# Hybrid decoder trunk: the sum over experts starts at zero, and each expert's rows bring half of the residual

## Chip, cores and metric

The kernel runs on one core of a Trainium2 chip. The metric is the device time of one execution in microseconds (us), the median over runs; all times here come from the profiler of the chip or from those runs.

## What is computed

The program is a decoder trunk of two layers over 512 tokens (four row tiles of 128) and 1024 columns, in float32. Each layer has a mixer with three kinds of attention (called `mix` here), a post-norm, a mixture of experts and a second post-norm:

```
for l in range(DEPTH):                       # DEPTH = 2, alpha = (2*DEPTH)**0.25
    mix = hybrid_mixer(x, ...)
    x = layer_norm(alpha * x + mix, ln1_g[l], ln1_b[l])
    moe = hier_moe(x, ...)                   # one group of 4, two experts of its 8
    x = layer_norm(alpha * x + moe, ln2_g[l], ln2_b[l])

# hier_moe, per token t, over 32 experts:
h = silu(t @ w_gate[e]) * (t @ w_up[e])      # 1024 -> 256
y = y + (h * gate[e]) @ w_down[e]            # 256 -> 1024; gate is zero but for two experts
```

Each token has exactly two experts with a gate that is not zero.

## The kernel before, in words

**Weights.** One expert has 3 MB of weights: two units of 1.5 MB, which `load_next` (L517 to L530) fetches with SP's DMA queue. Thirteen such units of SBUF form a ring; some of them (letters T and m of the ring, and the unit inside `xroom`) lie in rooms that attention used before. The ring is filled in the course of attention and the router; a further unit can only be loaded when the products that read its old content are done.

**End of attention.** For each of four row tiles, `out_proj` (its DVE instruction is L865) adds the output projection to the scaled residual in `yn[i]`. Statistics give mean and reciprocal deviation, ACT normalises the tile in place (L919), and ACT's queue writes it to `xd` in DRAM (L920). These rows are normalised, but without gain and bias.

**`first_rows`** (L885 to L890) then makes the residual of the second half of the layer: two VectorE (DVE) products over 128x1024, times the gain and plus the bias of the first norm (both in the tile `gb1`), and a DMA of 512 KB on ACT's queue into `y2` in DRAM. It works in place in `yn[i]`, so it waits until the DMA to `xd` has read that tile; only the fourth tile has a room of its own. It runs four times per layer. All experts add to `y2` later.

**Router** (L930 to L1098). A chain of small DVE instructions takes the best group (`gm`, `ghot`), the two best experts (`hot`, `selb`), the position of each token in its expert's list (`posm`) and one-hot rows (`oneh`, L1054); TensorE (PE) turns these into lists (`lists`), and `slot_rows` (L981 to L988) into row numbers `ri`.

**Pairs.** Two experts with up to 64 tokens each make a pair; there are 16 pairs per layer. GpSimd (POOL) gathers the 128 rows of a pair from `xd` by an indirect DMA into one of two rooms (`gathered`, DMA at L1000). `turned` (PE at L1011, DVE and ACT at L1017 and L1015) transposes them in eight PE instructions and applies gain and bias of the first norm on the way out of PSUM. 32 up products (`experts_up`), SiLU on ACT and a DVE product (`h`, L1032), two transposes and 16 down products (`experts_down`) follow. The two halves of the result leave PSUM scaled by the gate, one on ACT (L1044) and one on DVE (L1045), into one of three rooms (`row_room`), and POOL scatters the rows with an indirect DMA that adds to `y2` (L1046).

In the loop, `turned` of the next pair stands after `experts_mid` of the present pair and before its `experts_down`; the gather for two pairs later follows it. An `overflow` loop after the 16 pairs takes tokens beyond the 64 of an expert; in this profile it runs one item in layer 2 and none in layer 1.

**Second norm.** `gb2 = norm_rows(1)` (L243) loads gain and bias of the second norm, 1 MB broadcast, into the same tile as `gb1`. It stands in the text after pair 3, but the scheduler has put its DMA early on SP's queue, between weight loads (the order is shown below). After the last pair `y2` is read back (L1251), and the second norm uses `gb2` (L1263, L1265).

The scheduler keeps each engine's own stream in order: an instruction that waits holds all behind it on the same engine or queue.

Of the kernel before, what the change touches and what calls it, by code (L numbers as in the profile page):

```python
# [7 lines left out]
F32 = mybir.dt.float32  # L8
# [3 lines left out]
AF = mybir.ActivationFunctionType  # L12
# [52 lines left out]
def trunk(tc, a, out, dbg=None):  # L65
# [4 lines left out]
    with es:  # L70
# [177 lines left out]
        for l in range(DEPTH):  # L248
# [286 lines left out]

            dp = xhp.tile([128, 2 * NK * S], F32, name="dp", tag="xh")
# [366 lines left out]
            for i in range(NT):  # L903
# [17 lines left out]
                if i:  # L921
                    first_rows(i - 1)
# [96 lines left out]

            halves_ = ((0, 64), (64, 128))  # L1020

            def experts_up(xg, w):
                gu = bank("S")
                for k in range(NK):
                    for j, (c0, c1) in enumerate(halves_):
                        mm(gu[c0:c1], xg[:, k, c0:c1], gate_up(w[j], k), k == 0, k == NK - 1)
                return gu

            def experts_mid(gu):
                h = cp.tile([128, FH], F32, name="h", tag="rwg")  # L1030
                A.activation(h, gu[:, 0:FH], AF.Silu)  # L1031
                V.tensor_tensor(h, h, gu[:, FH:2 * FH], OP.mult)  # L1032
                return h

            def experts_down(h, w, rows):
# [13 lines left out]
            RI, XR, XG = {}, {}, {}  # L1049
# [49 lines left out]
            first_rows(NT - 1)  # L1099
# [4 lines left out]
            XG[0] = turned(XR.pop(0))  # L1104
# [31 lines left out]
            def overflow():  # L1136

                n_items = nc.values_load(eidi[0:1, MAX_ITEMS:MAX_ITEMS + 1], min_val=0, max_val=MAX_ITEMS)
                with tc.For_i(0, n_items) as item:
# [66 lines left out]
                    y = row_room()  # L1206
                    A.activation(y[0:64, 0:512], o[0:64], AF.Copy, scale=wr[0:64])
                    V.tensor_scalar(y[0:64, 512:1024], o[64:128], wr[64:128], None, op0=OP.mult)
# [3 lines left out]
            for p in range(NE // 2):  # L1212
# [9 lines left out]
                st = experts_down(h, w, RI.pop(p))  # L1222
# [9 lines left out]
            with tc.issue_after(last_on["PE"].ins), tc.issue_after(last_on["A"].ins), tc.issue_after(last_on["V"].ins), tc.issue_after(st.ins):  # L1232
# [12 lines left out]
            for j in range(2):  # L1245
                yu = carve(unit("A", "yt"), 0, [2, D])
# [8 lines left out]
            for i in range(NT):  # L1255
# [6 lines left out]
                for t, c in zip(src, halves):  # L1262
                    V.scalar_tensor_tensor(z[:, c], t, mv[:, 0:1], gb2[:, 0, c], op0=OP.subtract, op1=OP.mult)  # L1263
                for c in halves if i in (0, 3) else [slice(0, 1024)]:
                    V.scalar_tensor_tensor(z[:, c], z[:, c], mv[:, 2:3], gb2[:, 1, c], op0=OP.mult, op1=OP.add)  # L1265
# [77 lines left out]
```

## Time and profile before

| | us |
|---|---|
| runs | 1380.25, 1386.83, 1387.82 (median 1386.83) |
| profiled execution | 1385.0 |
| its span, first to last instruction | 1383.2 |

| engine | busy us | share of the span |
|---|---|---|
| PE (matmul) | 1194.4 | 86% |
| DVE | 696.6 | 50% |
| ACT | 442.9 | 32% |
| POOL | 292.5 | 21% |

In the rows further down, L888 is line 888 of the kernel; `yn<-yn,gb` names what an instruction writes and reads. SPq and ACTq are the DMA queues of SP and ACT. A bracket such as [4.74 <-DMA xd<-yn] gives the time for which the engine stood idle before the instruction, and what ended that. In views by stretches, the five busy times stand in the order PE, PEld (weight loads of PE), DVE, ACT, POOL; PEclk is the granted clock as a share of 2.4 GHz, and DMA the mean busy share of the 16 DMA engines.

### The profile page before, as it was taken

The page shows a single profiled execution, that of the slowest core. Times are in us where ns is not written, and L with a number is a line of the kernel's source. Part 1 is how long each engine was busy: PE and PEld are TensorE (multiplying, and loading weights), DVE is VectorE, ACT ScalarE, POOL GpSimd, SP SyncE. Part 2 cuts the span into 40 slices and gives each one's busy share as a digit, 9 for nine tenths or more (in the row PEclk, how much of TensorE's full clock was granted, in tenths as well). Part 3 has the DMA queues.
Part 4 walks back from the last instruction along what each step waited for, and adds up shares of the span by engine and source line. Part 5 has one row for each costly group of instructions (what it writes and reads, how often), then busy time and mean ns, then how long its engine had stood idle before and what let it go on. Part 6 is the DMA issues. An engine that isn't in the chain of part 4 may idle for free. (4 is left out here: it accounts for less than half of the span.)

```text
span 1383.2 us, 18273 instructions
## 1 busy us (share of the span) xinstructions
PE 1194.4 (86%) x6701; PEld 815.8 (59%) x6708; DVE 696.6 (50%) x1822; ACT 442.9 (32%) x1050; POOL 292.5 (21%) x286
## 2 busy tenths in 40 slices
PE   6989999999939989887599999999996699898860
PEld 6989976668924533222398899666795343332320
DVE  7599638684552422111668892668636333211125
ACT  3362256673102221111235322857611122111100
POOL 5332431201001121100332334230000122111011
PEclk9999999999969999999799999999998799999985
DMA  7321440115397999998552224200426899999943
GB/s 240 116 80 51 128 158 11 36 40 185 118 402 279 400 413 405 409 390 287 166 165 78 65 83 140 98 23 22 156 104 247 347 384 407 409 403 410 356 166 123
DMA packets 63898, 293.81 MB, mean 212 GB/s; under 512 B 16064, under 2 KB 20672, under 8 KB 48192
## 3 DMA queue, kind: packets, MB, share of 16 engines
q1 hardware_dynamic: 52128, 267.43, 50.5%
q0 software_dynamic: 9376, 16.81, 4.9%
q10 hardware_dynamic: 2304, 8.39, 1.5%
q8 instruction: 54, 0.88, 0.3%
q14 instruction: 36, 0.29, 0.1%
HBM read 278.06 MB, written 31.82 MB: 224 GB/s over the span
## 5 line engine op out<-in xcount | busy, mean ns | idle before, releaser
L97 PE MATMUL acc<-U,xh 128*128 128x384 f32 (+1 forms) x1584 | 298.9, 343 | 18.9 <-DVE xh L212 7.0
L97 PEld LDWEIGHTS acc<-U,xh 128*128 128x128 f32 x1584 | 280.5, 193 | 21.9 <-issue 6.9
L97 PE MATMUL S<-w,xg 128*64 128x512 f32 (+1 forms) x968 | 272.0, 608 | 10.6 <-DMA w<-w_e 8.9
L97 PEld LDWEIGHTS S<-w,xg 128*64 128x64 f32 x968 | 83.1, 141 | 138.8 <-issue 112.9
L1017 DVE TENSOR_SCALAR xg<-acc,lv 128x128 f32<-128x128 f32 x128 | 45.8, 404 | 179.6 <-PE S L97 142.9
L97 PE MATMUL o<-w,hT 128*64 128x512 f32 x488 | 125.4, 603 | 5.9 <-ACT hT L90 3.4
L199 POOL TENSOR_TENSOR U<-raw,U 128x768 fp32r<-128x768 f32 (+2 forms) x46 | 90.3, 1967 | 166.9 <-ACT U L196 166.9
L1046 POOL DMA_INDIRECT y<-xroom,ri x32 | 51.4, 1607 | 294.8 <-DVE xroom L1045 180.5
L1031 ACT ACTIVATE h<-S 128x256 f32<-128x256 f32 x32 | 12.3, 383 | 270.6 <-PE S L97 270.6
L196 ACT ACTIVATE U<-raw 128x768 fp32r<-128x768 f32 (+2 forms) x88 | 68.0, 812 | 71.6 <-PE acc L97 43.7
L1045 DVE TENSOR_SCALAR xroom<-o,rv 128x512 f32<-128x512 f32 x32 | 24.0, 751 | 117.7 <-PE o L97 117.7
L97 PEld LDWEIGHTS o<-w,hT 128*64 128x64 f32 x488 | 39.2, 138 | 67.1 <-issue 57.4
L1000 POOL DMA_INDIRECT xroom<-xd,ri x33 | 35.2, 1066 | 180.5 <-PE acc L1011 94.5
L199 DVE TENSOR_TENSOR U<-raw,U 128x768 fp32r<-128x768 f32 (+2 forms) x42 | 52.8, 1260 | 36.5 <-ACT U L196 34.0
L1011 PEld LDWEIGHTS acc<-cst,xroom 128*128 128x128 f32 x256 | 29.4, 147 | 60.6 <-issue 36.0
L90 ACT ACTIVATE uc<-T 128x512 f32<-128x512 f32 (+3 forms) x117 | 51.3, 460 | 40.9 <-PE T L297 39.1
L1015 ACT ACTIVATE xg<-acc,lv 128x128 f32<-128x128 f32 x128 | 48.9, 458 | 45.5 <-PE T L97 35.8
L1011 PE MATMUL acc<-cst,xroom 128*128 128x128 f32 x256 | 43.7, 298 | 22.7 <-DMA xroom<-xd,ri 20.7
L97 PE MATMUL acc<-U,oh 128*128 128x384 f32 (+1 forms) x384 | 63.3, 315 | 0.0
L1044 ACT ACTIVATE xroom<-o,rv 128x512 f32<-128x512 f32 x32 | 22.0, 687 | 111.0 <-PE o L97 111.0
L97 PEld LDWEIGHTS acc<-U,oh 128*128 128x128 f32 x384 | 56.8, 189 | 1.2 <-issue 1.0
L403 DVE MATCH_REPLACE8 uc<-m,uc 128x256 f32<-128x256 f32 (+2 forms) x96 | 51.4, 539 | 0.0
(367 smaller groups left out, 1942.0 us busy)
## 6 DMA issues: line engine op xcount, KB each, us to landing
w<-w_e SPq DMA_DIRECT2D x110, 1536.0 KB
raw<-w_in SPq DMA_DIRECT2D x64, 384.0 KB
xroom<-w_e SPq DMA_DIRECT2D x8, 1536.0 KB
w<-w_e SPq DMA_DIRECT2D x24, 512.0 KB
raw<-w_o SPq DMA_DIRECT2D x16, 384.0 KB
gb<-ln_rows SPq DMA_DIRECT2D x4, 1024.0 KB
xd<-yn ACTq DMA_DIRECT2D x8, 512.0 KB
y<-yn ACTq DMA_DIRECT2D x6, 512.0 KB
```

The costliest lines, as they stand in the source:

```text
L90: A.activation(o, i, AF.Copy, scale=1.0 if scale is None else scale)
L97: return PE.matmul(o, l, r, start=start, stop=stop, skip_group_check=True)
L196: A.activation(hi, r, AF.Copy)
L199: e.tensor_tensor(lo, r, hi.bitcast(F32), OP.subtract)
L403: V.match_replace(out=acc_t[i][:, :n], in_to_replace=m8, in_values=acc_t[i][:, :n], imm_value=TAKEN)
L1000: G.indirect_dma_start(out=xr[0:n], out_offset=None, in_=xd, in_offset=bass.IndirectOffsetOnAxis(ap=ri[0:n], axis=0), bounds_check=S - 1, ...
L1011: PE.transpose(t[:, 128 * j:128 * j + 128], xr[:, 128 * k:128 * k + 128], ident)
L1015: A.activation(xg[:, k], o, AF.Identity, scale=lv[:, 0, k, 0:1], bias=lv[:, 0, k, 1:2])
L1017: V.tensor_scalar(xg[:, k], o, lv[:, 0, k, 0:1], lv[:, 0, k, 1:2], op0=OP.mult, op1=OP.add)
L1044: last_on["A"] = A.activation(y[:, 0:512], o[0], AF.Copy, scale=rows[1])
L1045: last_on["V"] = V.tensor_scalar(y[:, 512:1024], o[1], rows[1], None, op0=OP.mult)
L1046: return G.indirect_dma_start(out=y2, out_offset=bass.IndirectOffsetOnAxis(ap=rows[0], axis=0), in_=y, in_offset=None, bounds_check=S - 1, ...
```

## The change

It does seven things.

1. `y2` is set to zero: POOL clears a 128x512 tile, and one SP DMA of 2 MB copies it over all of `y2`. This stands in the text after the first weight load, and in SP's order after the eighth load of attention's weights past the small norm tables, in each layer.
2. `gb1` is multiplied by 0.5 on ACT once per layer, 128x2048.
3. `first_rows` is gone, with its four calls.
4. `half_rows` is new: for each pair, two DVE products over 128x1024 make half of the residual from the gathered rows, in the room that the result will take. A token is gathered by two experts, so two halves add up.
5. Both halves of a pair's result now leave PSUM on DVE, in an instruction that also adds them to that room (`scalar_tensor_tensor`, 128x512).
6. `turned` of the next pair is issued after the last up product of the present pair, `half_rows` of the next pair after `h` of the present one, and the gather for two pairs later after that.
7. `gb2` comes in two DMAs of 512 KB after the last expert's weights, into units of the ring; the `overflow` loop uses `half_rows` on its 64 rows too.

```diff
+            y2 = dr.tile([S, D], F32, name="y2", tag="y2")
+            none = ring("P")
+            G.memset(none, 0.0)
+            SP.dma_start(y2.rearrange(...), none.unsqueeze(1).to_broadcast([128, 2 * NT, 512]))
...
             gb1 = norm_rows(0)
-            y2 = dr.tile([S, D], F32, name="y2", tag="y2")
-            def first_rows(i):
-                z = yn[i] if i < NT - 1 else at.tile([128, D], F32, name="x1", tag="u", bufs=3)
-                V.tensor_tensor(z, yn[i], gb1[:, 0], OP.mult)
-                V.tensor_tensor(z, z, gb1[:, 1], OP.add)
-                A.dma_start(y2[128 * i:128 * i + 128, :], z)
+            A.activation(gb1.rearrange("p a d -> p (a d)"), gb1.rearrange("p a d -> p (a d)"), AF.Copy, scale=0.5)
...
                 A.dma_start(xd[128 * i:128 * i + 128, :], z)
-                if i:
-                    first_rows(i - 1)
...
+            def half_rows(xr, n=128):
+                y = row_room()
+                V.tensor_tensor(y[0:n], xr[0:n], gb1[0:n, 0], OP.mult)
+                V.tensor_tensor(y[0:n], y[0:n], gb1[0:n, 1], OP.add)
+                return y
+            def next_half(p1):
+                if p1 in XR:
+                    with tc.issue_after(last_on["h"].ins):
+                        HR[p1] = half_rows(XR.pop(p1))
+                    fetch(p1 + 2)
...
                 transposes(hT.rearrange("p a b -> p (a b)"), [h[:, 0:128], h[:, 128:256]], 128)
+                next_half(p1)
...
-                y = row_room()
-                last_on["A"] = A.activation(y[:, 0:512], o[0], AF.Copy, scale=rows[1])
-                last_on["V"] = V.tensor_scalar(y[:, 512:1024], o[1], rows[1], None, op0=OP.mult)
+                for n in range(2):
+                    c = slice(512 * n, 512 * n + 512)
+                    last_on["V"] = V.scalar_tensor_tensor(y[:, c], o[n], rows[1], y[:, c], op0=OP.mult, op1=OP.add)
...
-            first_rows(NT - 1)
...
-            XG[0] = turned(XR.pop(0))
+            XG[0], HR[0] = turned(XR[0]), half_rows(XR.pop(0))
...
                 if p + 1 < NE // 2:
-                    XG[p + 1] = turned(XR.pop(p + 1))
-                    fetch(p + 3)
+                    with tc.issue_after(last_on["up"].ins):
+                        XG[p + 1] = turned(XR[p + 1])
...
-                    gb2 = norm_rows(1)
...
+            yus = [unit("A", "yt") for _ in range(2)]
+            gb2 = [yu[:, 2 * D:3 * D] for yu in yus]
+            for j in range(2):
+                SP.dma_start(gb2[j], a["ln_rows"][l:l + 1, 1, j].to_broadcast([128, D]))
```

SP's queue at the start of the experts of layer 1, before (`w` and `xroom` are weight units, `gb` the tile of both norms):

```order
L530 DMA w<-w_e 128x3072 x3
L530 DMA xroom<-w_e 128x3072
L530 DMA w<-w_e 128x3072
L243 DMA gb<-ln_rows 128x2048
L530 DMA w<-w_e 128x3072 x12
```

and with the change:

```order
L530 DMA w<-w_e 128x3072 x3
L530 DMA xroom<-w_e 128x3072
L530 DMA w<-w_e 128x3072 x13
```

The load of `gb`, behind which twelve weight loads stood, is no longer there; its two successors stand behind the last weight loads of the layer.

DVE around the router of layer 1, before (`Lg` are the router's scores, `x_3774` the room of the fourth tile):

```order
L932 TENSOR_REDUCE gm<-Lg 128x4
L888 TENSOR_TENSOR yn<-yn,gb 128x1024
L933 TENSOR_TENSOR ghot<-Lg,gm 128x16
L943 TENSOR_TENSOR pe__3649<-Lg,gm 128x16
L889 TENSOR_TENSOR yn<-yn,gb 128x1024
L935 TENSOR_TENSOR ghot<-ghot,cst 128x16
L888 TENSOR_TENSOR x_3774<-yn,gb 128x1024
L936 TENSOR_REDUCE sc_3641<-ghot 128x4
L889 TENSOR_TENSOR x_3774<-x_3774,gb 128x1024
L937 TENSOR_TENSOR ghot<-cst,sc_3641 128x16
```

and with the change:

```order
L928 TENSOR_REDUCE gm<-Lg 128x4
L929 TENSOR_TENSOR ghot<-Lg,gm 128x16
L939 TENSOR_TENSOR pe__3643<-Lg,gm 128x16
L931 TENSOR_TENSOR ghot<-ghot,cst 128x16
L932 TENSOR_REDUCE sc_3635<-ghot 128x4
L933 TENSOR_TENSOR ghot<-cst,sc_3635 128x16
```

The four products of `first_rows` between the router's small instructions are gone; the small ones keep their order.

DVE in the pair loop of layer 1, one pair before (`xg` are the transposed rows of the next pair, `rv`, `rr` and `ri` the lists of a later one):

```order
L1045 TENSOR_SCALAR xroom<-o,rv 128x512
L1032 TENSOR_TENSOR h<-h,S 128x256
L1017 TENSOR_SCALAR xg<-acc,lv 128x128 x4
L92 COPY hT<-T 128x256
L1067 COPY rv<-T 64x3
L1068 COPY rv<-T 64x3
```

and with the change:

```order
L1055 SCALAR_TENSOR_TENSOR xroom<-o,rv,xroom 128x512 x2
L1041 TENSOR_TENSOR h<-h,S 128x256
L1013 TENSOR_SCALAR xg<-acc,lv 128x128 x4
L92 COPY hT<-T 128x256
L1019 TENSOR_TENSOR xroom<-xroom,gb 128x1024
L1077 COPY rv<-T 64x3
L1020 TENSOR_TENSOR xroom<-xroom,gb 128x1024
L1078 COPY rv<-T 64x3
```

The two products of `half_rows` (L1019, L1020) stand behind `xg` and `hT`, ahead of the next copy out of `o`, and DVE has two copies out of `o` where it had one.

## Rows read from the trace of the kernel before

**Rows 1.** The page's chain that ended last, by line.

```profile
PE acc L97 8%; DMA w<-w_e 8%; PE S L97 5%; PE o L97 5%; PE T L297 2%; DMA xroom<-xd,ri 2%; DMA xd<-yn 1%; PE acc L1011 1%; ACT dp L566 1%; PE T L97 0%; ACT uc L90 0%; POOL mv L236 0%; DMA yt<-y 0%; DMA y<-xroom,ri 0%; DVE yt L1265 0%
```

**Rows 2.** Stretches, layer 1: from:to, length, busy per engine, PEclk, DMA, GB/s.

```profile
385.00:425.00 40.00, 16.94 (x83) 10.33 (x80) 19.80 (x89) 3.23 (x7) 3.78 (x3) 0.62 0.79 312
...
500.00:550.00 50.00, 45.28 (x207) 16.53 (x209) 10.45 (x33) 8.16 (x20) 8.39 (x7) 1.00 1.02 410
```

**Rows 3.** One shorter stretch of layer 1, the same columns.

```profile
416.00:426.00 10.00, 10.00 (x42) 3.82 (x42) 3.03 (x17) 3.17 (x6) 1.00 (x1) 0.79 0.24 58
```

**Rows 4.** The same view, layer 2.

```profile
1060.00:1100.00 40.00, 17.43 (x88) 10.92 (x89) 17.06 (x71) 3.83 (x9) 3.75 (x4) 0.62 0.81 315
...
1180.00:1230.00 50.00, 44.32 (x197) 15.32 (x193) 11.12 (x35) 8.00 (x20) 8.91 (x7) 1.00 1.02 407
```

**Rows 5.** SP queue waits, 330 to 690: total us, times, longest.

```profile
SPq L530 <- DMA w<-w_e: 133.5, 39, 5.8
...
SPq L243 <- DVE ghot L937: 9.8, 1, 9.8
```

**Rows 6.** Timeline of PE, layer 1: start, us, instruction [idle <-releaser].

```profile
651.77 1.93 PE L97 MATMUL S<-w,xg 128*64 128x512 f32 x6 [1.55 <-DMA w<-w_e]
```

**Rows 7.** Timeline of DVE around the router of layer 1.

```profile
382.76 0.17 DVE L932 TENSOR_REDUCE gm<-Lg 128x4 f32<-128x16 f32 x1
387.66 1.23 DVE L888 TENSOR_TENSOR yn<-yn,gb 128x1024 f32<-128x1024 f32 x1 [4.74 <-DMA xd<-yn]
```

**Rows 8.** Timeline of POOL, layer 1.

```profile
403.73 1.78 POOL L1000 DMA_INDIRECT xroom<-xd,ri  x1 [21.48 <-DVE ri L986]
405.82 1.00 POOL L1000 DMA_INDIRECT xroom<-xd,ri  x1 [0.31 <-DVE rv L1068]
...
434.98 1.63 POOL L1046 DMA_INDIRECT y<-xroom,ri  x1 [7.17 <-issue]
```

**Rows 9.** Timeline of DVE around the router of layer 2.

```profile
1055.92 0.17 DVE L932 TENSOR_REDUCE gm<-Lg 128x4 f32<-128x16 f32 x1
...
1067.73 1.22 DVE L888 TENSOR_TENSOR yn<-yn,gb 128x1024 f32<-128x1024 f32 x1 [5.30 <-DMA xd<-yn]
```

**Rows 10.** The chain of waits, 1040 to 1100: start, us, what.

```profile
1056.13 11.58 DMA xd<-yn
...
1077.57 10.06 DMA xroom<-xd,ri
```

**Rows 11.** Timeline of ACT and its queue, layer 1.

```profile
378.25 0.33 ACTq L920 DMA_DIRECT2D xd<-yn  x1
...
382.91 1.24 ACT L919 ACTIVATE yn<-yn,mv 128x1024 f32<-128x1024 f32 x1 [4.69 <-DVE mv L918]
384.18 0.33 ACTq L920 DMA_DIRECT2D xd<-yn  x1
```

**Rows 12.** Waits of all engines, 385 to 690: total us, times, longest.

```profile
PE T L297 <- DVE h L1032: 9.9, 10, 1.0
```

**Rows 13.** Timeline of DVE in the pair loop, layer 1.

```profile
451.24 0.42 DVE L1032 TENSOR_TENSOR h<-h,S 128x256 f32<-128x256 f32 x1 [4.91 <-ACT h L1031]
...
453.21 0.42 DVE L1054 TENSOR_TENSOR oneh<-posm,cst 128x256 fp32r<-128x256 f32 x1
```

**Rows 14.** Timeline of DVE in the tail of layer 2.

```profile
1328.68 0.75 DVE L1045 TENSOR_SCALAR xroom<-o,rv 128x512 f32<-128x512 f32 x1 [6.22 <-PE o L97]
...
1339.41 0.69 DVE L1188 TENSOR_TENSOR xg<-acc,lv 128x512 f32<-128x512 f32 x1 [4.63 <-PE acc L1185]
...
1362.52 0.74 DVE L1263 SCALAR_TENSOR_TENSOR yt<-yt,mv,gb 128x512 f32<-128x512 f32 x1
```

**Rows 15.** Timeline of ACT there.

```profile
1327.82 0.69 ACT L1044 ACTIVATE xroom<-o,rv 128x512 f32<-128x512 f32 x1 [4.40 <-PE o L97]
```

**Rows 16.** The stretch in which the changed order puts the zero fill.

```profile
70.00:96.00 26.00, 24.27 (x130) 23.50 (x131) 23.07 (x50) 19.60 (x51) 3.00 (x3) 0.93 0.12 40
```

**Rows 17.** All instructions on y2: their DMAs, issue to landing.

```profile
DMA to landing us min/median/max: 6.8/10.5/12.0
```

More of the change, by code (lines that the diff above doesn't have):

```diff
@@ L533, in trunk @@
             load_next()
+            y2 = dr.tile([S, D], F32, name="y2", tag="y2")
+            none = ring("P")
+            G.memset(none, 0.0)
+            SP.dma_start(y2.rearrange("(p r) c -> p (r c)", r=NT).rearrange("p (n c) -> p n c", c=512), none.unsqueeze(1).to_broadcast([128, 2 * NT, 512]))
             dp = xhp.tile([128, 2 * NK * S], F32, name="dp", tag="xh")
@@ L1025, in experts_up @@
                     for j, (c0, c1) in enumerate(halves_):
-                        mm(gu[c0:c1], xg[:, k, c0:c1], gate_up(w[j], k), k == 0, k == NK - 1)
+                        last_on["up"] = mm(gu[c0:c1], xg[:, k, c0:c1], gate_up(w[j], k), k == 0, k == NK - 1)
                 return gu
@@ L1031, in experts_mid, with experts_down @@
                 A.activation(h, gu[:, 0:FH], AF.Silu)
-                V.tensor_tensor(h, h, gu[:, FH:2 * FH], OP.mult)
+                last_on["h"] = V.tensor_tensor(h, h, gu[:, FH:2 * FH], OP.mult)
                 return h
-            def experts_down(h, w, rows):
+            def experts_down(h, w, rows, y, p1):
                 hT = cp.tile([128, 2, 128], F32, name="hT", tag="rw")
                 transposes(hT.rearrange("p a b -> p (a b)"), [h[:, 0:128], h[:, 128:256]], 128)
+                next_half(p1)
                 o = [bank("o") for _ in range(2)]
@@ L1205, in overflow @@
                             mm(o[c], hT[:, f], down(w, f, h), f == 0, f == 1)
-                    y = row_room()
-                    A.activation(y[0:64, 0:512], o[0:64], AF.Copy, scale=wr[0:64])
-                    V.tensor_scalar(y[0:64, 512:1024], o[64:128], wr[64:128], None, op0=OP.mult)
+                    y = half_rows(xr, 64)
+                    V.scalar_tensor_tensor(y[0:64, 0:512], o[0:64], wr[0:64], y[0:64, 0:512], op0=OP.mult, op1=OP.add)
+                    V.scalar_tensor_tensor(y[0:64, 512:1024], o[64:128], wr[64:128], y[0:64, 512:1024], op0=OP.mult, op1=OP.add)
                     G.indirect_dma_start(out=y2, out_offset=bass.IndirectOffsetOnAxis(ap=ri[0:64], axis=0), in_=y[0:64], in_offset=None,
@@ L1217, in trunk @@
                 if p + 1 < NE // 2:
-                    XG[p + 1] = turned(XR.pop(p + 1))
-                    fetch(p + 3)
+                    with tc.issue_after(last_on["up"].ins):
+                        XG[p + 1] = turned(XR[p + 1])
                 if p % 2 == 0 and p // 2 + 2 < NE // 4:
                     lists(p // 2 + 2)
-                st = experts_down(h, w, RI.pop(p))
+                st = experts_down(h, w, RI.pop(p), HR.pop(p), p + 1)
                 load_next()
@@ L1228, in trunk @@
                     pieces()
-                    gb2 = norm_rows(1)
             last = l == DEPTH - 1
-            with tc.issue_after(last_on["PE"].ins), tc.issue_after(last_on["A"].ins), tc.issue_after(last_on["V"].ins), tc.issue_after(st.ins):
+            yus = [unit("A", "yt") for _ in range(2)]
+            gb2 = [yu[:, 2 * D:3 * D] for yu in yus]
+            for j in range(2):
+                SP.dma_start(gb2[j], a["ln_rows"][l:l + 1, 1, j].to_broadcast([128, D]))
+            with tc.issue_after(last_on["PE"].ins), tc.issue_after(last_on["V"].ins), tc.issue_after(st.ins):
                 if not last:
@@ L1245, in trunk @@
             for j in range(2):
-                yu = carve(unit("A", "yt"), 0, [2, D])
+                yu = carve(yus[j], 0, [2, D])
                 for i in range(2):
@@ L1262, in trunk @@
                 for t, c in zip(src, halves):
-                    V.scalar_tensor_tensor(z[:, c], t, mv[:, 0:1], gb2[:, 0, c], op0=OP.subtract, op1=OP.mult)
+                    V.scalar_tensor_tensor(z[:, c], t, mv[:, 0:1], gb2[0][:, c], op0=OP.subtract, op1=OP.mult)
                 for c in halves if i in (0, 3) else [slice(0, 1024)]:
-                    V.scalar_tensor_tensor(z[:, c], z[:, c], mv[:, 2:3], gb2[:, 1, c], op0=OP.mult, op1=OP.add)
+                    V.scalar_tensor_tensor(z[:, c], z[:, c], mv[:, 2:3], gb2[1][:, c], op0=OP.mult, op1=OP.add)
                 if last:
```

2 lines of the change are left out of this document (1 added, 1 removed).

## The prediction, made before the changed kernel had run

> **What bounds the kernel now.** I read the page's chain first [rows 1]. Attention's products (PE acc) and the expert weights (DMA w<-w_e) have 8% each; `DMA xd<-yn`, 1%, and `DMA xroom<-xd,ri`, 2%, belong to the passage from attention to the experts, which the change touches. So I read the experts by stretches [rows 2, 4]. Between 500 and 550 us the DMA engines are full (1.02, 410 GB/s), and so are they between 1180 and 1230 (1.02, 407 GB/s). PE looks nearly full too (45.28 of 50 us), but SP's queue says who leads: its weight loads waited 133.5 us in 39 waits for earlier weight loads [rows 5], and the last up products of layer 1 waited 1.55 us for weights [rows 6]. In the experts' main part the time is bytes over bandwidth. Work that PE, DVE or ACT is spared there is worth nothing, and work added there costs nothing while the loads stay full.
>
> The passage before it is another matter. From 385 to 425 PE is busy 16.94 of 40 us and from 1060 to 1100 17.43 of 40 [rows 2, 4], and from 416 to 426 the DMA engines are almost empty (0.24, 58 GB/s) [rows 3]: the ring of units is full, and the next loads wait for the first pair's products. When the first pair starts sets when the stream of weights resumes, and by bytes over bandwidth the stream then ends as much earlier. So the question is how much earlier the first gather can start.
>
> **The chain from the router to the first gather.** In layer 1 the router's first instruction (`gm`) starts at 382.76; the next stands behind a `first_rows` product that waited 4.74 us for the DMA that writes `xd` [rows 7]. The first gather starts at 403.73 [rows 8], 20.97 us after `gm`. In between lie that wait and four products of `first_rows` (the order shows them), each 1.23 us like the one in [rows 7]. All are in DVE's own stream: 4.74 + 4 × 1.23 = 9.7 us. In layer 2 `gm` is at 1055.92, the wait is 5.30 us [rows 9], and the gather starts at 1077.57 [rows 10]: 21.65 us. Again four products lie between: 5.30 + 4 × 1.22 = 10.2 us. Without them 11.3 us and 11.5 us are left, the same chain in both layers, as it must be; I take that as a check of the reading.
>
> **Term 1, `first_rows` gone: −9.7 and −10.2 us.** What is late next? The gather reads `xd`, so it waits for the fourth tile's DMA. In layer 1 the third was issued at 378.25 [rows 11] and released the product at 387.66 [rows 7], 9.4 us later; in layer 2 such a DMA took 11.58 us [rows 10]. The fourth was issued at 384.18 [rows 11]: landed at about 393.6, against a gather at 403.73 − 9.7 = 394.0. It just fits. Four products lie before `gm` too and may make the router 0 to 2.4 us earlier (two of 1.2 us in the last tile's time); since the DMA's landing is then the limit, I count 0. From the other side, twelve weight loads no longer wait behind the load of `gb` (9.8 us [rows 5]) and will share the engines with these DMAs. Against that, the four 512 KB writes of `y2` leave ACT's queue, where they stood between the writes of `xd`. Bounds for the two layers together: −10 us (half is taken back by the landing) to −25 us. I keep −19.9, which is nearest to the rows.
>
> **Term 2, bytes out of the passage: 0.** 2 MB of `y2` and 1 MB of `gb` go from a stretch with 312 GB/s; but the ring runs full and the engines fall idle afterwards [rows 3], so this only lengthens the idle time.
>
> **Term 3, zero fill: 0.** One POOL instruction and one DMA of 2 MB, where the engines are busy 0.12 [rows 16]; at the 407 GB/s of a full stretch [rows 4] it takes 5 us. Behind it on SP stand loads of attention's weights; between 70 and 96 they have room. If that cover is gone it costs up to 5 us once per layer.
>
> **Term 4, `gb1` halved on ACT: +0.5.** 128x1024 took 1.24 us [rows 11], so 2.5 us per layer. In layer 1 it stands between copies out of PSUM early in attention and must wait for the load of `gb1`. Bounds 0 and 5 us for two layers; most is covered by PE's queue of products.
>
> **Term 5, the pairs: 0.** Per pair DVE gets two products (2 × 1.22) and a second copy out of `o` (0.74, like the instruction of that kind in [rows 14]): 3.2 us more. Between 500 and 550 DVE was busy 10.45 us for 3.3 pairs of 15 us [rows 2], about 3.2 us per pair, so it comes to 6.4 of 15 us. The cover is DVE's idle time. The second copy adds no wait at a pair's end: the first bank was free for ACT at 1327.82 [rows 15], the second for DVE at 1328.68 [rows 14]; one engine can do one after the other. The transposes behind the up products fill PE's wait for `h`, 9.9 us in ten waits [rows 12], but in the full stream this is worth 0 (bounds: 0 and −20 us in two layers).
>
> Do DVE's added products and POOL's gathers block each other? The trace shows a gather of 1.78 us at 403.73 and one of 1.00 us at 405.82 [rows 8], the latter beside one-hot products with two SBUF inputs; such a product took 0.42 us beside no POOL work [rows 13]. I see no lock there. The Trainium skill, page "SBUF — State Buffer", section "Who interferes with whom", says that a DVE instruction with two SBUF inputs contends with a GpSimd instruction that reads SBUF, the later one being blocked fully. By it, each gather, released by the first product of `half_rows`, would block or be blocked by the second; the trace does not agree, and it stands below as a rival.
>
> **Term 6, overflow: +1.2.** In layer 2's tail one product of `half_rows` stands between the two `xg` instructions (the first at 1339.41 [rows 14]), and up products wait for both: 1.22 us.
>
> **Term 7, `gb2` at the end: 0.** 1 MB after the last weights, 2.6 us at 407 GB/s; the first loads of the next layer come that much later, while the last products and the last scatter run.
>
> **Sum.** −9.7 − 10.2 + 0.5 + 1.2 = −18.2 us. The profiled execution took 1385.0 us, so 1366.8; the median of the runs shown is 1.8 us above it, 1386.8 − 18.2 = 1368.6. I say **1368.5 us**, 1.3% less. A measurement of this kernel tells about 0.5%, 6.9 us, from no change: the border of faster is 1379.9, of slower 1393.8.
>
> **Rivals.**
> - *Half is taken back by the landing of `xd`.* For it: the two waits of the products show 9.4 and 11.58 us of landing on full engines [rows 7, 10, 11], and the weight loads now come earlier. Against it: ACT's queue carries half the bytes. At −10 + 1.7: about 1378.5.
> - *The DVE stream becomes the bound.* This is the one on the slower side, and its place is `half_rows` in the loop. Its room is that of the scatter three pairs back. The first scatter started at 434.98 [rows 8], and the DMAs land after 10.5 us, at most 12.0 [rows 17], so at 447.0; `half_rows` of pair 3 comes behind `h` of pair 2 (451.24) and its `xg`, so by 453 [rows 13]. That is 6 us of slack. If landings took more than 18 us, or if DVE fell behind PE, each microsecond of delay per pair would be 32 us over 32 pairs: at 1 us, 1368.6 + 32 = about 1400. Against it: 6.4 of 15 us busy.
> - *DVE and POOL block each other.* The second product of `half_rows` and the gather that the first one releases come at the same time in each pair. If one waits for the other, that is about a gather's 1.00 us [rows 8] per pair on DVE; with 32 pairs and DVE on the path, 1368.6 + 32 = about 1400. Against it: the gather beside one-hot products took no longer, nor did the products [rows 8, 13], and the gather is for two pairs later. This is what the rule of the Trainium skill in term 5 would lead to.
> - *The start does not matter.* If the stream of weights were held by something at its end, such as the last scatter, both layers would end as before: 1386.8 + 1.7 = 1388.5. Against it: [rows 5, 6].
> - *PE's waits for `h` count.* If PE and not the loads set the pace, 20 us more go: about 1350. Against it: 1.02 of DMA share.
>
> **How the numbers follow.** Forecast 0.68, with its own range 1360 to 1377; half taken back 0.13; start without effect 0.08; DVE bound 0.04; DVE and POOL blocking each other 0.02; PE's waits 0.05. Low end 1355, a part of the way to the last rival and the −25 bound; high end 1380, which takes in the first rival. Left out are the start without effect, both cases of a slow DVE and about half of the PE case, 0.17. Faster by over 0.5%: 0.68 + 0.05 + two thirds of 0.13 = 0.82. Within 0.5%: 0.08 + the rest = 0.12. Slower: 0.06.
>
> **What would show it.** Right: the first gather about 11.4 us after `gm` in both layers; no DVE wait for `xd<-yn`; no 9.8 us wait of SP before the weights; the empty stretch of DMA just as long, but some 10 us earlier; pairs still 15 us in the full stretches; DVE busy some 80 us more (32 × 3.2 − 8 × 2.4), ACT some 17 us less (32 × 0.69 − 2 × 2.5). Wrong: a gather that waits on POOL's queue for `xd`; a DMA share below 0.95 in the middle of the experts; PE waiting for DVE there.

## The result and the profile after

The changed kernel takes 1364.38 us (median of four runs, 1363.18 to 1367.05), beside 1386.34 us for the kernel before in the same comparison: ratio 0.9857, 95% interval [0.9828, 0.9886]. The forecast was 1368.5 us. The profiled execution took 1363.18 us; its span is 1361.4 us, against 1383.2.

The trace cut at landmarks of the pairs (`gm` is the router's first instruction):

| stretch | before | after | difference | forecast |
|---|---|---|---|---|
| start to the first router logits `lt`, layer 1 | 365.28 | 364.29 | −1.0 | +0.25 |
| to `gm`, layer 1 | 17.48 | 16.03 | −1.45 | 0 |
| `gm` to the first gather, layer 1 | 20.97 | 11.77 | −9.2 | −9.7 |
| first gather to the last scatter, layer 1 | 257.15 | 256.53 | −0.6 | 0 |
| last scatter to `gm`, layer 2 | 395.04 | 392.60 | −2.4 | +0.25 |
| `gm` to the first gather, layer 2 | 21.65 | 12.60 | −9.05 | −10.2 |
| first gather to the last pair's scatter, layer 2 | 252.61 | 253.28 | +0.7 | 0 |
| to the scatter of the overflow item | 22.03 | 23.64 | +1.6 | +1.2 |
| to the end | 30.99 | 30.66 | −0.3 | 0 |
| sum | 1383.2 | 1361.4 | −21.8 | −18.2 |

So 18.25 of 21.8 us lie in the two passages from the router to the gather. The page of the kernel after, its line of busy times and its chain by line:

```profile
PE 1183.1 (87%) x6708; PEld 822.5 (60%) x6708; DVE 776.5 (57%) x1905; ACT 425.6 (31%) x1019; POOL 299.1 (22%) x288
...
PE acc L97 9%; DMA w<-w_e 8%; PE S L97 7%; PE o L97 5%; PE T L297 2%; DMA y<-xroom,ri 1%; DMA xroom<-xd,ri 1%; PE acc L1007 1%; ACT dp L572 1%; DMA yt<-y 0%; PE T L97 0%; ACT uc L90 0%; DVE xg L1013 0%; DVE yt L1277 0%; POOL mv L236 0%
```

`DMA xd<-yn`, 1% in [rows 1], is gone from the chain. DVE is busy 79.9 us more and ACT 17.3 us less, as the forecast had it (80 and 17). DVE at the router and POOL's gathers, layer 1:

```profile
380.32 0.17 DVE L928 TENSOR_REDUCE gm<-Lg 128x4 f32<-128x16 f32 x1
380.53 0.17 DVE L929 TENSOR_TENSOR ghot<-Lg,gm 128x16 f32<-128x16 f32 x1
```

```profile
392.09 1.79 POOL L996 DMA_INDIRECT xroom<-xd,ri  x1 [12.44 <-DVE ri L982]
394.19 1.01 POOL L996 DMA_INDIRECT xroom<-xd,ri  x1 [0.31 <-DVE rv L1078]
404.99 1.00 POOL L996 DMA_INDIRECT xroom<-xd,ri  x1 [9.79 <-DVE xg L1013]
417.63 1.39 POOL L996 DMA_INDIRECT xroom<-xd,ri  x1 [11.65 <-DVE rr L981]
422.31 1.64 POOL L1056 DMA_INDIRECT y<-xroom,ri  x1 [3.29 <-DVE xroom L1055]
```

`gm`'s successor follows after 0.2 us; the wait of 4.74 us and the four products of [rows 7] are gone, and the first gather starts at 392.09 instead of 403.73 [rows 8]. The same stretches as in [rows 2, 4], and one short one in place of [rows 3]:

```profile
385.00:425.00 40.00, 28.17 (x129) 14.07 (x127) 19.65 (x71) 5.29 (x12) 6.82 (x5) 0.79 0.86 341
408.00:412.00 4.00, 4.00 (x22) 1.26 (x18) 0.00 (x0) 0.00 (x0) 0.00 (x0) 1.00 0.21 39
500.00:550.00 50.00, 41.50 (x195) 18.95 (x193) 20.16 (x48) 5.94 (x16) 8.10 (x7) 1.00 1.01 411
1060.00:1100.00 40.00, 36.57 (x169) 15.65 (x170) 18.41 (x46) 7.23 (x17) 7.54 (x5) 0.90 0.84 321
1180.00:1230.00 50.00, 41.46 (x176) 15.55 (x178) 18.21 (x39) 5.95 (x16) 7.89 (x6) 0.93 1.02 412
```

In the middle of the experts the DMA engines move 411 and 412 GB/s, as before; DVE is busy 20.16 of 50 us there instead of 10.45, and the DMA engines stay full. In the passage PE is busy 28.17 of 40 us instead of 16.94. The almost empty stretch of the DMA engines is 4 us long in layer 1 (0.21), where it was 10 us (0.24); for layer 2 see term 2 below.

What still ends the passage is seen on DVE, whose first product of `half_rows` waits for the gathered rows:

```profile
402.72 1.23 DVE L1019 TENSOR_TENSOR xroom<-xroom,gb 128x1024 f32<-128x1024 f32 x1 [7.14 <-DMA xroom<-xd,ri]
```

The gather was issued at 392.09, so its rows took 10.6 us. Before the change PE got them at 414.14, 10.4 us behind the gather at 403.73. The forecast had not looked at this landing; the last group of experiments is about it.

### The profile page after: what moved, and what is told of

Read it like the earlier page. It is cut to its first block, busy times and chain, and to the rows that moved or that the text cites. A ratio compares the mean times of both kernels' runs of the same rounds, so it can differ in the third digit from the quotient of the medians.

```text
span 1361.4 us, 18270 instructions
## 1 busy us (share of the span) xinstructions
PE 1183.1 (87%) x6708; PEld 822.5 (60%) x6708; DVE 776.5 (57%) x1905; ACT 425.6 (31%) x1019; POOL 299.1 (22%) x288
## 5 line engine op out<-in xcount | busy, mean ns | idle before, releaser
L97 PE MATMUL acc<-U,xh 128*128 128x384 f32 (+1 forms) x1584 | 294.8, 339 | 20.5 <-DVE xh L212 7.2
L97 PEld LDWEIGHTS acc<-U,xh 128*128 128x128 f32 x1584 | 275.3, 190 | 24.6 <-ACT U L196 7.2
L97 PEld LDWEIGHTS S<-w,xg 128*64 128x64 f32 x968 | 91.5, 141 | 171.2 <-issue 100.3
L97 PE MATMUL o<-w,hT 128*64 128x512 f32 x488 | 134.2, 615 | 7.5 <-ACT hT L90 3.9
L1041 DVE TENSOR_TENSOR h<-h,S 128x256 f32<-128x256 f32 x32 | 13.5, 421 | 189.4 <-ACT h L1040 189.4
L996 POOL DMA_INDIRECT xroom<-xd,ri x33 | 40.6, 1230 | 275.6 <-issue 142.7
L97 PEld LDWEIGHTS o<-w,hT 128*64 128x64 f32 x488 | 43.6, 140 | 73.9 <-issue 51.0
L1055 DVE SCALAR_TENSOR_TENSOR xroom<-o,rv,xroom 128x512 f32<-128x512 f32 x64 | 48.0, 750 | 56.3 <-PE o L97 52.3
L1007 PE MATMUL acc<-cst,xroom 128*128 128x128 f32 x256 | 38.6, 299 | 14.3 <-DMA xroom<-xd,ri 14.3
## 6 DMA issues: line engine op xcount, KB each, us to landing
w<-w_e SPq DMA_DIRECT2D x24, 512.0 KB, 17.3
```

The source lines that it names most:

```text
L97: return PE.matmul(o, l, r, start=start, stop=stop, skip_group_check=True)
L996: G.indirect_dma_start(out=xr[0:n], out_offset=None, in_=xd, in_offset=bass.IndirectOffsetOnAxis(ap=ri[0:n], axis=0), bounds_check=S - 1, ...
L1007: PE.transpose(t[:, 128 * j:128 * j + 128], xr[:, 128 * k:128 * k + 128], ident)
L1055: last_on["V"] = V.scalar_tensor_tensor(y[:, c], o[n], rows[1], y[:, c], op0=OP.mult, op1=OP.add)
```

## Experiments

Each kernel is the changed one with the edit shown, but for e5 and e6, which start from the kernel before. The kernel before ran beside each on the same chip; its median was between 1383.0 and 1386.3 us in these comparisons, so a distance of 3 us between kernels of different comparisons is at the edge of what can be told, and there the traces' stretches are read beside it. Lines of an edit that only give an instruction a name (`last_on["ri"] = ...`, `wrote = ...`, `last_on["g"] = ...`, `ready = ...`) are left out of the diffs.

### Does the start set the end?

**e1_four_products** puts four idle DVE products with two inputs between the router's instructions:

```diff
-            V.tensor_tensor(pe_, ...)
+            first = V.tensor_tensor(pe_, ...)
+            idle = at.tile([128, D], F32, name="x1", tag="u", bufs=3)
+            with tc.issue_after(first.ins):
+                for j in range(4):
+                    late = V.tensor_tensor(idle, gb1[:, 0], gb1[:, 1], OP.mult)
```

(`selb` comes behind `late`.)

> The changed kernel with four idle DVE products of 128x1024 between gm and selb in each layer's router, in the places that first_rows had; no wait and no DMA comes back. Theory (the first gather's start sets when the weight stream resumes, and so the end): the first gather 4.5 to 4.9 us later in each layer, and the time 1364.4 + 9 to 10 = about 1374. Rival (the landing of xd or the weight stream holds the passage anyway): the gathers move, the time rises by 2 us or less, 1364 to 1366.

1372.85 us, ratio 0.9928 [0.99, 0.9956]: 8.5 us above the changed kernel. From `gm` to the gather it takes 16.18 and 16.13 us, 4.41 and 3.53 us more; from there to the last scatters 256.15 and 253.16 us, as in the changed kernel (256.53, 253.28). A delay of the first gather reaches the end in full. The idle tile has a side effect that e9b below explains: three weight loads wait until 388.6 for it. It does not spoil the reading, since the ring was full again at 410.29, before the next load could go out at 417.38.

**e2_three_mb** writes 3 MB to DRAM on ACT's queue behind the last write of `xd`:

```diff
+            junk = dr.tile([6 * 128, D], F32, name="junk", tag="junk")
+            with tc.issue_after(wrote.ins):
+                A.dma_start(junk.rearrange("(p r) c -> p r c", r=6), gb1[:, 0].unsqueeze(1).to_broadcast([128, 6, D]))
```

> The changed kernel with one more DMA of 3 MB per layer on ACT's queue behind the last write of xd, from SBUF to a DRAM tile that nobody reads: the bytes that the change took out of the passage, without their waits. The prediction's term 2 says 0: the ring runs full before the first products free a unit, so 1364.4. Rival, from the trace of the changed kernel: the fill's last load lands at 407.8 and the first unit is free at 410.8, so only 3 us of 7.5 us are covered, and 4.5 us per layer show: about 1373.5. If it also slows the first gather's landing, more.

1367.79 us, ratio 0.9888 [0.986, 0.9916]: 3.4 us above the changed kernel: clearly not 9, and at the edge of what can be told from 0. Its stretches in layer 1:

```profile
402.00:412.00 10.00, 6.68 (x30) 3.74 (x32) 4.06 (x7) 2.79 (x5) 1.00 (x1) 0.67 1.01 421
412.00:422.00 10.00, 10.00 (x52) 3.86 (x50) 6.24 (x21) 2.27 (x6) 1.39 (x1) 1.00 1.03 431
```

The empty stretch is filled (1.01, 1.03), and most of the bytes fit into it; between the first gather and the last scatter 1.2 and 2.3 us are added in the two layers. The rows of the first gather are there 10.9 us after its issue in layer 1 and 10.8 us in layer 2, instead of 10.6 and 9.6.

### Would it have been enough to move `first_rows`?

**e5_first_later** is the kernel before, with all four `first_rows` behind the row numbers of the first two gathers:

```diff
-                if i:
-                    first_rows(i - 1)
...
-            first_rows(NT - 1)
+            with tc.issue_after(last_on["ri"].ins):
+                for i in range(NT):
+                    first_rows(i)
```

> The kernel before with all of first_rows moved behind the row numbers of the first two gathers on DVE; everything else as before, so its 2 MB on ACT's queue and the load of gb ahead of the weight loads on SP stay. Theory of the prediction (only DVE's chain counts): the gathers 9 to 10 us earlier in each layer, 1386.3 - 19 = about 1367. Rival (the weight loads behind gb start some 8 us later, at about 400, and the bytes stay): the stream resumes only when this fill has landed, at about 420 instead of 424 in layer 1, 1386.3 - 8 = about 1378.

1393.4 us, ratio 1.007 [1.0049, 1.0091]: slower than before. POOL and DVE:

```profile
394.31 10.80 POOL L998 DMA_INDIRECT xroom<-xd,ri  x1 [11.84 <-DVE ri L984]
405.42 1.00 POOL L998 DMA_INDIRECT xroom<-xd,ri  x1 [0.31 <-issue]
```

```profile
394.13 2.35 DVE L888 TENSOR_TENSOR yn<-yn,gb 128x1024 f32<-128x1024 f32 x2
396.40 2.35 DVE L889 TENSOR_TENSOR yn<-yn,gb 128x1024 f32<-128x1024 f32 x2
398.68 1.22 DVE L888 TENSOR_TENSOR yn<-yn,gb 128x1024 f32<-128x1024 f32 x1
...
403.22 0.75 DVE L1052 TENSOR_TENSOR oneh<-posm,cst 128x256 fp32r<-128x256 f32 x2
```

The gather starts early, but its instruction lasts 10.80 us instead of 1: it is held until DVE's row of products with two SBUF inputs is over (403.97), and then takes its microsecond.

**e6_first_after_lists** moves `first_rows` behind the second batch of lists too, so that the first two gathers run free (the diff is against e5):

```diff
+            lists(1)
             with tc.issue_after(last_on["ri"].ins):
                 for i in range(NT):
                     first_rows(i)
...
-            lists(1)
```

> As e5, but first_rows stands on DVE behind the row numbers of the second list as well, so that the first two gathers are issued before its products start; its 2 MB and the load of gb ahead of the weight loads on SP stay. In e5 the first gather's instruction lasted 10.80 us beside eight products with two SBUF inputs. If that lock alone made e5 slow and only the start counts: first gather about 11.5 us after gm, instruction under 2 us, last scatter of layer 1 257 us after the gather, time 1384 - 19 = about 1365 to 1368. Rival (the weight loads that stand behind gb, now from about 406, and the bytes take the gain back): gather early all the same, but last scatter 262 to 267 us after it, time 1375 to 1386.

1384.16 us, ratio 1.0012 [0.9999, 1.0026]: no difference. The first gather starts 11.5 us after `gm`, but from it to the last scatters it takes 267.65 and 263.42 us, some 10 us more than before. The products now stand ahead of pair 0's `xg`, they hold the third gather (7.42 us instead of 1), and SP's load of `gb`, which waits for them, goes out at 408.13 with the weight loads behind it. So moving the products within the passage gave nothing as long as the load of `gb` waited for them; which of the two, the products' new place or that load, costs how much, e6 does not separate.

### The parts in the pair loop

**e4_half_twice** does the two products of `half_rows` twice:

```diff
+                for j in range(2):
+                    V.tensor_tensor(y[0:n], xr[0:n], gb1[0:n, 0], OP.mult)
+                    V.tensor_tensor(y[0:n], y[0:n], gb1[0:n, 1], OP.add)
```

> The changed kernel with both products of half_rows written twice for each pair and for the overflow item, 2.4 us more of DVE per pair. Theory (weights set the pace, DVE is cover): nothing from the 32 pairs, up to 2.4 us at each layer's first pair and 2.4 us in the overflow item, 1365 to 1371. Rival (DVE's stream is the bound of the pairs): up to 32 x 2.4 = 78 us, 1390 or more.

1367.76 us, ratio 0.9884 [0.9853, 0.9915]. DVE is busy 851.1 us instead of 776.5. These 74.6 us of DVE cost 3.4 us in the medians, and 2.9 and 0.8 us from the first gather to the last scatters (259.46 and 254.09). DVE's idle time is the cover, as term 5 had it.

**e3_turned_early** puts the transposes back where they were:

```diff
-                    with tc.issue_after(last_on["up"].ins):
-                        XG[p + 1] = turned(XR[p + 1])
+                    XG[p + 1] = turned(XR[p + 1])
```

> The changed kernel with the transposes of the next pair in their old place, not held back behind the last up product. Theory (weights set the pace): PE waits for h again, some 10 us per layer, the stretch from first gather to last scatter keeps its 257 and 253 us within 2 us, time 1363 to 1367. Rival (PE's waits count): up to 20 us more, 1375 to 1384.

1439.06 us, ratio 1.0423 [1.038, 1.0466]: 75 us above the changed kernel. Both expectations fell. Between 400 and 690 us PE waited for (total us, times, longest):

```profile
PE acc L1007 <- DMA xroom<-xd,ri: 36.9, 10, 6.9
PE T L297 <- DVE h L1041: 10.9, 11, 1.0
```

the same between 1090 and 1390 us:

```profile
PE acc L1007 <- DMA xroom<-xd,ri: 48.4, 10, 7.4
```

and the DMA engines at the end of layer 1:

```profile
600.00:650.00 50.00, 39.00 (x160) 13.19 (x156) 13.66 (x23) 4.61 (x14) 8.03 (x5) 0.97 0.87 323
640.00:690.00 50.00, 36.53 (x156) 12.02 (x155) 13.23 (x21) 4.88 (x12) 5.36 (x5) 0.91 0.37 100
```

`half_rows` reads the gathered rows, so the gather for two pairs later can only be issued behind it, and that is behind `h` of the present pair. Transposes that the scheduler places among the present pair's up products then wait for rows that have not landed, with up products behind them on PE. The units are released late, and the DMA share falls: 0.91 from 550 to 600 us, where the changed kernel has 1.01, and then 0.87. In the changed kernel only pair 0's transposes wait for gathered rows (one wait of 6.9 us in layer 1, one of 7.4 in layer 2), those behind up products never. The added waits, 30.0 and 41.0 us, are about what the stretches from the first gather to the last scatters grow by, 29.4 and 43.0 us. That part of the change is what makes the others possible.

**e7_tail_order** puts `half_rows` of the overflow item behind both `xg`:

```diff
-                    V.tensor_tensor(xg, xg, gb[1], OP.add)
+                    turn = V.tensor_tensor(xg, xg, gb[1], OP.add)
...
-                    y = half_rows(xr, 64)
+                    with tc.issue_after(turn.ins):
+                        y = half_rows(xr, 64)
```

> The changed kernel with one order altered: in the overflow item of layer 2, half_rows comes behind both xg instructions instead of between them. Theory (the 1.6 us that the overflow item gained is one product of half_rows, 1.21 us, ahead of the second xg, plus the wait it makes): from the last gather to the overflow scatter 18.36 - 1.2 to 1.6 = about 17 us (16.63 before the change), the rest as in the changed kernel, so 1363 us, less than a measurement tells from 1364.4. Rival (the product is only moved: it then stands between up and down products and delays the scatter as much): 18.4 us, 1364.4.

1364.73 us, ratio 0.986 [0.984, 0.9879]: no difference in the median. In the trace the gather stands at 1315.78 and the overflow scatter at 1332.11: 16.33 us instead of 18.36, so the tail does gain 2.0 us, less than runs differ by. In the changed kernel the order was:

```profile
1315.50 1.22 DVE L1019 TENSOR_TENSOR xroom<-xroom,gb 64x1024 f32<-64x1024 f32 x1 [3.92 <-DMA xroom<-xd,ri]
1316.67 0.69 DVE L1197 TENSOR_TENSOR xg<-acc,lv 128x512 f32<-128x512 f32 x1
1317.28 1.21 DVE L1020 TENSOR_TENSOR xroom<-xroom,gb 64x1024 f32<-64x1024 f32 x1
1318.41 0.68 DVE L1198 TENSOR_TENSOR xg<-xg,lv 128x512 f32<-128x512 f32 x1
```

Both products of `half_rows` stand ahead of the second `xg`, not one as term 6 counted.

### What holds the gather: inputs from SBUF

**e8_two_inputs** adds four idle products behind the row numbers of the first list:

```diff
+            idle = at.tile([128, D], F32, name="x1", tag="u", bufs=3)
+            with tc.issue_after(last_on["ri"].ins):
+                for j in range(4):
+                    V.tensor_tensor(idle, gb1[:, 0], gb1[:, 1], OP.mult)
```

> The changed kernel with four idle DVE products of 128x1024 with both inputs in SBUF right behind the row numbers of the first list, where the first gather is issued. If a product with two SBUF inputs that is running holds POOL's gather back, and the next one in the queue does too, the gather's instruction lasts until the run of such products is over, 4 to 6 us instead of 1.8, and lands as much later. Rival (e5's gather was long for another reason, such as full DMA queues): under 2 us.

**e9_one_input** has `V.tensor_reduce(out=idle[:, j:j + 1], in_=gb1[:, 0], ...)` in place of each product.

> As e8, with four DVE reductions over 128x1024, which have one SBUF input, in place of the products. If two inputs in SBUF are what holds the gather, its instruction now lasts 1.0 to 1.8 us. Rival (any busy DVE holds it): 4 to 6 us as in e8.

One run each: 1365.94 and 1359.61 us. POOL in e8:

```profile
391.45 5.19 POOL L996 DMA_INDIRECT xroom<-xd,ri  x1 [12.59 <-DVE ri L982]
```

POOL and DVE in e9:

```profile
394.79 1.27 POOL L996 DMA_INDIRECT xroom<-xd,ri  x1 [11.78 <-DVE ri L982]
```

```profile
394.61 0.15 DVE L982 SCALAR_TENSOR_TENSOR ri<-rv,rr 128x1 int32<-128x1 f32 x1
394.68 4.59 DVE L1112 TENSOR_REDUCE x<-gb 128x1 f32<-128x1024 f32 x4
```

Beside products with two SBUF inputs the gather takes 5.19 us; beside reductions, which have one, 1.27. The reductions also write only 128x1, which e9 does not separate from the number of inputs; a gather of the changed kernel that ran beside `xg`, which is read from PSUM and written to SBUF (128x128), took 1.04 us (493.34, last section). e9 was also faster than the changed kernel, which neither theory had said.

### Who gets the DMA engines first

**e9b_one_input_timed** is e9 again, in five runs.

> The kernel of e9 again (four idle DVE reductions with one SBUF input behind the row numbers), now timed: its one look gave 1359.6 us, less than any run of the changed kernel, though it only adds 4.6 us of DVE work per layer. Theory (run variation, the added work lies in DVE's wait for the gathered rows): 1364, no difference from the changed kernel that can be told. Rival (the later one-hot products and third gather leave the DMA engines to the first gather, which landed in 5.8 instead of 10.6 us): 1360, 4 us under the changed kernel, and the first gather's landing again under 7 us.

1358.85 us, ratio 0.9815 [0.9793, 0.9836], while e7 in the same comparison stood at 0.986 [0.984, 0.9879]: the gain is real. The idle tile lies in attention's room `u`, from which a unit of the ring is taken later, so SP's weight load into that unit waited for the reductions, and with it two loads behind it, until 399.32. The second gather, issued at 396.35, landed in 4.3 us.

**e10_lists_later** changes DVE's order alone: the second batch's one-hot products behind both row numbers (and e7's order).

```diff
-            lists(1)
+            with tc.issue_after(ready.ins):
+                made = hots(1)
+            lists(1, made)
```

> The order of e7 and, in each layer, the one-hot products of the second batch of lists behind the row numbers (ri) of the first two gathers, so that no DVE instruction with two SBUF inputs runs when the first gather starts. Theory: the first gather takes 1.0 instead of 1.79 us (1.15 in layer 2) and, since the rows then land some 0.8 and 0.1 us earlier at most, the time falls by under 1 us to about 1362. Rival (DVE's later one-hot products hold the third gather and pair 0's xg, as the products of e6 did): third gather 1 to 2 us later, 1365.

1363.09 us, ratio 0.9842 [0.9826, 0.9858]: no difference that can be told. The first gather still met a one-hot product and took 1.51 us; none was running as the second started, which took 1.01 us, yet it landed 12.0 us after its issue. DVE's order alone does not bring the gain.

**e11_loads_held** holds the loads without any work on DVE:

```diff
+            held = at.tile([128, D], F32, name="x1", tag="u", bufs=3)
             for p in range(2):
                 fetch(p)
+            with tc.issue_after(last_on["g"].ins):
+                G.memset(held[:, 0:1], 0.0)
```

> The changed kernel and, in each layer, one POOL memset of 128x1 behind the first two gathers, into a tile of the room from which the next weight load but two takes its unit: those loads can then be issued only when the two gathers are. No DVE work is added. Theory (e9b was 5.5 us faster than the changed kernel because its idle tile held SP's last weight loads until behind the gathers, so that the gathers landed in 4 to 6 instead of 10 us; the reductions themselves did nothing): first gather lands within 6 us in both layers, the almost empty stretch of DMA before the second release of weights is gone, 1357 to 1360 us. Rival (what helped was DVE's order: no product with two SBUF inputs beside the second gather): 1364, with loads that then are short at the first pairs, 1366.

1357.43 us, ratio 0.9798 [0.9785, 0.9812], the fastest of all: 7 us under the changed kernel, whose interval lies wholly above. DVE in layer 1:

```profile
398.52 1.23 DVE L1019 TENSOR_TENSOR xroom<-xroom,gb 128x1024 f32<-128x1024 f32 x1 [2.19 <-DMA xroom<-xd,ri]
```

SP's queue over the whole run, and the stretches:

```profile
SPq L530 <- POOL x L1111: 30.9, 2, 17.5
```

```profile
385.00:425.00 40.00, 32.67 (x165) 16.07 (x166) 23.03 (x82) 7.17 (x17) 6.92 (x6) 0.87 0.98 386
408.00:412.00 4.00, 4.00 (x25) 1.97 (x22) 2.26 (x11) 1.89 (x5) 0.00 (x0) 1.00 1.00 402
1060.00:1100.00 40.00, 40.00 (x198) 16.63 (x196) 22.02 (x57) 5.94 (x16) 8.81 (x6) 1.00 1.00 396
```

With the gather at 392.84 the rows are there after 5.7 us instead of 10.6, in layer 2 after 4.1 instead of 9.6. SP waits 30.9 us in two waits for the memset, and yet the empty stretch is gone (1.00 at 408 to 412): loads that went out early only filled the ring and then waited for the first pair, and on the way they shared the DMA engines with the gather. DVE's order is as in the changed kernel, and the first gather still meets a product (1.78 us), so e11 leaves the loads as the cause. One side effect remains: as in e9b, the small load of `rb` for the next layer moves ahead on SP's queue. Between the first gather and the last scatters 2.9 and 5.2 us are saved.

## Why the prediction was right, step by step

- **What bounds the kernel.** Right, and shown: e1's delay came out at the end in full, e4's 74.6 us of DVE nearly not at all.
- **Term 1.** Right to 0.5 and 1.1 us (−9.2 and −9.05 against −9.7 and −10.2). In layer 2 the gather started 0.85 us after the fourth write of `xd` had landed (11.7 us behind its issue). That is the limit that the forecast feared: e8, e9 and e11 show the same 0.85 to 0.86 us, and in e9 the trace names the write as what ended POOL's wait:

```profile
1055.37 1.15 POOL L996 DMA_INDIRECT xroom<-xd,ri  x1 [14.19 <-DMA xd<-yn]
```

So in layer 2 a gather did wait for `xd`, one of the forecast's signs of being wrong, but it cost about 1 us (12.60 us behind `gm` instead of the forecast's 11.5); the first rival, half of the gain, did not happen. "I count 0" for an earlier `gm` was the mis-sized term. From the first `lt` of a layer to `gm`:

| us | before | e5 | e6 | after |
|---|---|---|---|---|
| layer 1 | 17.48 | 16.05 | 16.04 | 16.03 |
| layer 2 | 16.44 | 15.51 | 15.52 | 15.52 |

Up to `gm`, e5 and e6 differ from the kernel before only in that `first_rows` is gone from there, so the 1.45 and 0.92 us are shown to be its price, inside the bounds that the forecast gave (0 to 2.4). The forecast fell short by 3.6 us in the profiled executions (18.2 against 21.8). Most of the rest lies in attention, where the traces differ by more than that: the first `lt` of layer 1 comes at 363.5 to 368.4 us in them, and from the last scatter of layer 1 to the first `lt` of layer 2 they take 376.3 to 379.9 us.
- **Term 2.** "This only lengthens the idle time" failed in layer 1. From 414 to 426 us the DMA engines of the kernel before are idle for 8.9 of 12 us, from 405 to 413 those of the changed kernel for 4.5 of 8; the last load of the fill landed at 407.76, only 3.1 us before the next could go out (410.83). In layer 2 the idle time stayed, 4.5 and 4.2 us. The four stretches, before and after:

```profile
414.00:426.00 12.00, 11.86 (x49) 5.68 (x50) 3.74 (x18) 3.17 (x6) 1.00 (x1) 0.74 0.26 70
1091.00:1099.00 8.00, 8.00 (x37) 2.73 (x34) 1.65 (x8) 1.85 (x3) 0.00 (x0) 0.90 0.44 141
```

```profile
405.00:413.00 8.00, 8.00 (x37) 2.76 (x38) 1.82 (x4) 2.92 (x6) 0.98 (x1) 0.93 0.44 133
1066.00:1075.00 9.00, 9.00 (x42) 3.31 (x38) 1.93 (x5) 2.61 (x5) 0.66 (x1) 0.88 0.53 169
```

The term counted the idle time as cover without asking whether it is long enough: 3 MB take some 7.7 us at the 410 GB/s of [rows 2] (an estimate), more than what is left in either layer. e2 puts 3 MB back in each layer and finds about 3.5 us for the two together, little more than runs differ by. The later landing of the first gather is 0.3 us of it in layer 1 and 1.3 us in layer 2; the rest is not explained. The landing is also what the forecast left out: it followed the chain to the gather's start only, and keeping other loads out of that landing was worth 7 us (e11).
- **Terms 3, 4 and 7.** Their stretches hold −1.0 (start to `lt`) and −0.3 us (to the end), no more than runs differ by, so a cost of a few us there would not be seen. The halving of `gb1` waits 3.04 us for its load and takes 1.92 us:

```profile
45.70 1.92 ACT L889 ACTIVATE gb<-gb 128x2048 f32<-128x2048 f32 x1 [3.04 <-DMA gb<-ln_rows]
```

- **Term 5.** The sum, 0, was right (−0.6 and +0.7), and two reasons under it were wrong. That "in the full stream this is worth 0" may hold for the transposes' old wait for `h`, but their new place carries the later gather: without it 75 us are lost (e3). The forecast took them as a part by itself, without asking for what the gather waits once `half_rows` reads its room.
- "I see no lock there" was wrong. In [rows 8] the gather of 1.78 us is the lock itself: a one-hot product with two SBUF inputs was running as it started. The gather of 1.00 us at 405.82 started 0.11 us ahead of such a product. DVE there, in the kernel before:

```profile
403.62 0.75 DVE L1054 TENSOR_TENSOR oneh<-posm,cst 128x256 fp32r<-128x256 f32 x2
...
405.93 0.41 DVE L1054 TENSOR_TENSOR oneh<-posm,cst 128x256 fp32r<-128x256 f32 x1
```

In the changed kernel a gather that meets the running second product takes longer (1.39 us at 417.63), and e5, e8 and e9 show that it is held. The Trainium skill's "SBUF — State Buffer", section "Who interferes with whom", says that the later of the two is blocked fully; where the gather is the later one the runs agree (10.80 us against 1), where DVE's product is, they don't (1.21 us at 493.80, last section). The rival's price failed all the same: POOL is the one that waits, the gather is for two pairs later, and the product stays at 1.21 to 1.22 us.
- **Term 6.** +1.6 instead of +1.2 us: two products, not one, stood ahead of the second `xg` (e7).
- **The DVE rival** did not come: 20.16 of 50 us busy, DMA share 1.01.

## What to carry to other kernels

Where a stream of loads sets the pace, follow the chain of its first consumer through the landing of what it waits for, not only to its issue: a load that is issued early only to wait for that consumer later does harm if it is under way together with the consumer's own small transfer, and one ordering point that holds it back was worth 7 us here. Work that only finishes something for later, like the residual here, is better put out of such a passage altogether; moved within it, with a load waiting for it, it took back all that it gave (e6). Parts of a change must be costed together when one moves the release of a buffer that another waits for (e3).

## What the runs showed of the hardware

- A gather by POOL that starts while DVE runs instructions with two SBUF inputs is held. In e5 and e8 it waited for the whole row of them: 10.80 us behind some 9.8 us of products, and 5.19 us. DVE's one-input reductions did not hold it (1.27 us in e9).
- It does not always wait for the whole row. At 1079.07 in the changed kernel it waited for the running product alone, and ended at 1080.98 while four one-hot products, which have two SBUF inputs as well, were still running. What lets it in there and not in e5 and e8 is open.

```profile
1079.07 1.91 POOL L996 DMA_INDIRECT xroom<-xd,ri  x1 [12.40 <-DVE hT L92]
```

```profile
1078.89 1.22 DVE L1020 TENSOR_TENSOR xroom<-xroom,gb 128x1024 f32<-128x1024 f32 x1
1080.03 1.42 DVE L1064 TENSOR_TENSOR oneh<-posm,cst 128x256 fp32r<-128x256 f32 x4
```

- In the other order nothing is held: a gather that started at 493.34 took 1.04 us, and the product that started 0.46 us after it took 1.21 us. At 1170.00 the product came 0.15 us behind the gather, with the same 1.04 and 1.21 us.

```profile
493.34 1.04 POOL L996 DMA_INDIRECT xroom<-xd,ri  x1 [8.46 <-issue]
```

```profile
492.84 1.04 DVE L1013 TENSOR_SCALAR xg<-acc,lv 128x128 f32<-128x128 f32 x3
493.80 1.21 DVE L1020 TENSOR_TENSOR xroom<-xroom,gb 128x1024 f32<-128x1024 f32 x1
```

- The 512 KB of rows of the first two gathers landed 9.6 to 12.9 us after the issue in the changed kernel, with weight loads under way, and 3.4 to 6.5 us after it where three loads of 1.5 MB were held back (e9, e9b, e11) or the weight loads stood behind `gb` (e6). They share the engines rather than wait their turn: the gather of 392.09 landed at 402.70, ahead of a weight load issued at 379.52 (404.04).
